# Value quads in the first layer, one-by-one takeover of accumulators, and eight adjoining runs of quads in the down projections

## The chip, the cores and the metric

The kernel runs on one core of one Trainium2 chip. The metric is the time on the device in microseconds: the median of three runs before the change is 2054.72 us (2054.33 to 2054.86).

TensorE (PE in the profile) multiplies; VectorE (DVE) and ScalarE (ACT) prepare what it reads and take over what it sums up in its eight PSUM banks; SyncE (SP) and GpSimd (POOL) issue most of the transfers.

## What is computed

Two transformer layers on 256 tokens of width 2048, in float32. The first layer has block-sparse attention, which for 256 tokens is plain causal attention in one block; the second has sliding-window attention with grouped keys and values. Both have a convolutional feed-forward network of inner width 5504.

```python
q, k, v = jnp.split(x @ w_qkv, 3, axis=-1)      # first layer, 2048 -> 3 x 2048
...
h = layer_norm(ALPHA * h + attn, ln_g[layer, 0], ln_b[layer, 0])
ffn = conv_ffn(h, ffn_w_up[layer], ffn_conv_w[layer], ffn_conv_b[layer], ffn_w_down[layer])
h = layer_norm(ALPHA * h + ffn, ln_g[layer, 1], ln_b[layer, 1])
...
return (jax.nn.gelu(g) * v) @ w_down            # 5504 -> 2048, at the end of conv_ffn
```

## The kernel before

**Products in three parts.** Every float32 operand is split into a high part that TensorE takes at its fast rate and a low remainder. A product of a 128-row block with a 512-column block is three matmuls (L530 to L532: high by high, high by low, low by high).

**The weight stream.** Weights come as *halves* of 128 x 1024 numbers (512 KB), all in one fixed sequence through all stages. SP loads a half into one of six `raw` buffers (L141). ACT copies its high part to `wh` (L160), DVE subtracts to get `wl` (L169), and when that is done the next load is issued. Four pairs `wh`, `wl` exist, so a half's split can begin when PE has finished the half four before it. Splits are called three halves ahead of their use.

**Stages.** For each layer: the attention's projections with the attention itself between them (value groups of 512 columns, and a unit for each head's query and key), the output projection, the up projection (86 units), the down projection. A stage with moving weights takes its output in two *chunk pairs* c = 0, 1 of 2 x 512 columns each (n = 0, 1 and n = 2, 3) and two token tiles t = 0, 1.

**Quads.** A *plain* half holds two weight blocks, each used for both token tiles: 4 block products, 12 matmuls. A *quad* treats 2 row blocks by 2 column blocks by 2 token tiles as a 2 x 2 product and needs 7 products instead of 8. A *run* is two quads in 7 halves of two products each (the list `SEVEN`); four of the seven hold weight blocks as they are, the halves that begin with T1 and T2 hold sums of weight blocks. `PLAINS` and `PLAINS_O` give the number of plain halves between the runs. A pair with quads uses all eight banks: four `acc` banks for (n, t) and four `at` banks for P1, P5, P6, P7, which `fold` adds up afterwards with DVE.

**Sums of weights** are made ahead by `presums`: two loads of 512 KB, four DVE steps (L436) and two stores to DRAM through POOL (L440) per quad, at given *slots*. **Sums of the source** are made on the spot by `sums`: `whole` (L588), `combine` (L599), `split` (L604, L605).

**What sets the order.** The engines run their own lists in the order in which the program writes them. The program counts slots: `step` closes one, `at(n, f)` puts `f` n slots later, and those actions are written at the next `take` of a half, right behind the splits called there. In the down projections a slot is one half.

**Ends of chunks and stages.** `evac` takes a finished bank into the residual `res` (L547, L549) and the last part of a (t, n) is followed by statistics (L553). Here it is called when both token tiles of an n are done. The last eight halves of a stage are the *window*: all eight for t = 0, then all eight for t = 1, so that the norm of t = 0 (`moments`, `norm`, L611 to L623) and its transposes (`turn`, L632, and `low`, L639) run beside the second pass. For this the window's splits are kept in spare places (`homes`, in `xT`, `st` and `up`), and in layer 0's down projection a table `reach` calls the splits further and further ahead, up to six halves of the next stage.

## Time and profile before

| | |
|---|---|
| median of three runs | 2054.72 us |
| the profiled execution | 2053.82 us |
| its span, first to last instruction | 2052.1 us |
| granted TensorE clock | 0.998 |
| `wl` splits on DVE (L169), one of 128 x 1024 | 1223 ns |
| `wh` splits on ACT (L160), one of 128 x 1024 | 1054 ns |
| quad steps ahead (L436), one of 224 | 685 ns |
| moved by DMA | 566.64 MB, mean 276 GB/s |

The profile is one execution, read by an engine's busy time, by the wait that ended an idle time, and by the granted clock. A matmul's row lasts about 390 ns, but matmuls overlap: the distance from one start to the next is the rate. Rows of the profile are named by line and operation, output and inputs; the line numbers are those of the kernel before.

### The profile page before, as it was taken

What the parts mean: (1) busy time and instruction counts of PE and PEld (TensorE: products, weight loads), DVE (VectorE), ACT (ScalarE), POOL (GpSimd) and SP (SyncE); (2) the same over time, 40 slices, a digit from 0 to 9 for tenths busy, and PEclk for the clock granted to TensorE, in tenths of its full rate; (3) what the DMA queues carried; (4) which work ended last, traced back from release to release, by engine and by line L of the source; (5) the groups of instructions that cost most, each with busy time, mean ns of one, the idle gap of its engine ahead of it and who ended that gap; (6) DMA issues with size and microseconds to landing.
All of it is one profiled execution on the core that took longest, in us unless ns stands there. A gap on an engine that the chain in (4) does not pass through costs nothing.

```text
span 2052.1 us, 29718 instructions
## 1 busy us (share of the span) xinstructions
PE 2036.1 (99%) x10908; PEld 1759.3 (86%) x10908; DVE 1675.9 (82%) x2399; ACT 1138.3 (55%) x1676; POOL 75.4 (4%) x138
## 2 busy tenths in 40 slices
PE   9999999999999999999999999999999999999997
PEld 7888888988888888888888888898888888888886
DVE  5676678888888888899896788978888888889887
ACT  5444456455555555566673556545555555556672
POOL 0100000000000000000000000000000000000000
PEclk9999999999999999999999999999999999999999
DMA  8888988468888888888994767838888888889893
GB/s 297 287 281 328 320 287 313 162 238 282 289 288 273 282 296 269 285 286 329 323 366 156 261 217 252 285 126 275 281 286 283 279 283 291 272 266 328 312 361 150
DMA packets 158722, 566.64 MB, mean 276 GB/s; under 512 B 19008, under 2 KB 21376, under 8 KB 157296
## 3 DMA queue, kind: packets, MB, share of 16 engines
q1 hardware_dynamic: 136064, 492.74, 70.7%
q0 software_dynamic: 20160, 69.64, 8.7%
q10 hardware_dynamic: 2352, 2.36, 0.3%
q8 instruction: 86, 1.41, 0.3%
q14 instruction: 60, 0.49, 0.1%
HBM read 503.78 MB, written 65.06 MB: 277 GB/s over the span
## 4 chain that ended last, share of the span: by engine, by line
PE 98%; DVE 1%; DMA 0%; ACT 0%; issue 0%; ACTq 0%; DVEq 0%
PE acc L322 39%; PE acc L324 20%; PE acc L530 7%; PE acc L531 7%; PE acc L532 7%; PE at L532 2%; PE at L531 2%; PE at L530 2%; PE acc L386 2%; PE acc L385 2%; PE acc L387 2%; PE acc L349 1%; PE acc L361 1%; PE at L722 1%; PE at L755 1%; PE at L748 1%
## 5 line engine op out<-in xcount | busy, mean ns | idle before, releaser
L169 DVE TENSOR_TENSOR wl<-raw,wh 128x1024 fp32r<-128x1024 f32 (+1 forms) x754 | 898.8, 1220 | 186.4 <-ACT wh L160 163.9
L160 ACT ACTIVATE wh<-raw 128x1024 fp32r<-128x1024 f32 (+1 forms) x754 | 770.4, 1052 | 207.9 <-PE acc L532 104.5
L322 PE MATMUL acc<-xT,wh 128*128 128x512 f32 x3456 | 832.8, 392 | 0.0
L322 PEld LDWEIGHTS acc<-xT,wh 128*128 128x128 f32 x3456 | 641.1, 188 | 128.6
L324 PEld LDWEIGHTS acc<-xT,wl 128*128 128x128 f32 x3456 | 444.2, 190 | 12.4
L324 PE MATMUL acc<-xT,wl 128*128 128x256 f32 x3456 | 452.5, 284 | 0.0
L909 ACT ACTIVATE h<-acc 128x256 f32<-128x256 f32 x172 | 66.4, 386 | 409.1 <-PE acc L324 203.1
L917 DVE SCALAR_TENSOR_TENSOR c<-h,cw,c 128x255 f32<-128x255 f32 x344 | 165.4, 481 | 9.1 <-ACT c L913 2.8
L436 DVE TENSOR_TENSOR gb<-gb 128x512 f32<-128x512 f32 x224 | 153.5, 685 | 5.9 <-DMA gb<-in_wsum_dram 5.9
L910 DVE TENSOR_TENSOR h<-acc,h 128x256 f32<-128x256 f32 x172 | 72.7, 423 | 64.2 <-ACT h L909 64.2
L440 POOL DMA_DIRECT2D ws<-gb x112 | 59.8, 534 | 1412.1 <-DVE gb L436 1360.3
L530 PE MATMUL acc<-wh,up 128*128 128x512 f32 x275 | 107.0, 389 | 0.0
L531 PE MATMUL acc<-wl,up 128*128 128x512 f32 x275 | 107.0, 389 | 0.0
L532 PE MATMUL acc<-wh,up 128*128 128x512 f32 x275 | 107.0, 389 | 0.0
L913 ACT ACTIVATE c<-h,cw 128x256 f32<-128x256 f32 x172 | 101.7, 591 | 0.0
L530 PE MATMUL acc<-wh,st 128*128 128x512 f32 x174 | 68.8, 395 | 0.0
L531 PE MATMUL acc<-wl,st 128*128 128x512 f32 x174 | 67.8, 390 | 0.0
L532 PE MATMUL acc<-wh,st 128*128 128x512 f32 x174 | 67.8, 390 | 0.0
L831 ACT ACTIVATE qT<-acc 128x256 f32<-128x256 f32 x32 | 12.3, 385 | 91.3 <-PE acc L324 65.9
L532 PEld LDWEIGHTS acc<-wh,up 128*128 128x128 f32 x275 | 51.6, 188 | 10.7
L530 PEld LDWEIGHTS acc<-wh,up 128*128 128x128 f32 x275 | 51.6, 188 | 10.7
L531 PEld LDWEIGHTS acc<-wl,up 128*128 128x128 f32 x275 | 51.6, 188 | 10.6
(193 smaller groups left out, 2152.5 us busy)
## 6 DMA issues: line engine op xcount, KB each, us to landing
raw<-in_wst_dram SPq DMA_DIRECT2D x694, 512.0 KB, 5.2
gb<-in_wsum_dram SPq DMA_DIRECT2D x112, 512.0 KB, 7.6
ws<-gb POOLq DMA_DIRECT2D x112, 512.0 KB, 6.2
raw<-ws SPq DMA_DIRECT2D x112, 512.0 KB, 5.6
bias<-band POOLq DMA_DIRECT2D x8, 512.0 KB, 7.2
band<-ud POOLq DMA_DIRECT2D x4, 512.0 KB, 12.7
band<-ud ACTq DMA_DIRECT2D x4, 512.0 KB
res<-in_x_dram SPq DMA_DIRECT2D x2, 1024.0 KB, 9.4
```

The costliest lines, as they stand in the source:

```text
L160: nc.scalar.activation(wh[:, c], raws[s][:, c], AF.Copy)
L169: nc.vector.tensor_tensor(out=wl[:, c], in0=raws[s][:, c], in1=wh[:, c].bitcast(F32), op=ALU.subtract)
L322: nc.tensor.matmul(acc, w, xT[:, k, :], start=(k == 0), stop=(k == ends[0]))
L324: nc.tensor.matmul(acc[:, 0:T], w, xT[:, k, 0:T], start=False, stop=(k == ends[1]))
L436: nc.vector.tensor_tensor(out=w[:, o:o + 512], in0=a, in1=b, op=op)
L530: nc.tensor.matmul(acc, sh, wh, start=first, stop=False)
L531: nc.tensor.matmul(acc, sh, wl, start=False, stop=False)
L532: nc.tensor.matmul(acc, sl, wh, start=False, stop=last)
L909: nc.scalar.activation(h, acc[:, T:2 * T], AF.Copy)
L910: nc.vector.tensor_tensor(out=h, in0=acc[:, 0:T], in1=h, op=ALU.add)
L913: nc.scalar.activation(c, h, AF.Identity, bias=w[:, 3:4], scale=w[:, 2:3])
L917: nc.vector.scalar_tensor_tensor(c[:, d:T], h[:, 0:T - d], w[:, 2 - d:3 - d], c[:, d:T], op0=ALU.mult, op1=ALU.add)
```

## The change

**Value quads.** In the first layer the third and fourth value groups are taken as one chunk pair by the new `v_pair`, with two runs of quads as in an output projection (8 plain halves and 14 of runs, 22 in place of 16). Its source sums go to rows of `st` that are still unused. Four more quads are summed ahead for it.

**Down projections.** In the second chunk pair there are eight runs instead of six, one behind the other, and then 11 plain halves (before: 42 halves of runs with 4 plain ones between, then 15 plain). The source sums of the two new runs are made within this chunk pair, at slots 9, 12, 14 and 15 and again 14 slots later, and are written over the blocks of runs 4 and 5, which therefore come first. Of the 11 plain halves eight are the window. Eight more quads are summed ahead; those of the down projections are now nearly all made during the up projections (26 and 27 of them, before 20 and 20), about every 6 slots instead of 8.

**Takeover.** `evac` is called for each (n, t) as it is done, and at slot distance 0, or 1 for t = 1 of odd n in the down projections (before: 1 and 2 for odd n). Since n = 2 now reaches into the window, `late` takes it over there.

The helpers of quads (`target`, `product`, `fold`, `sums`) move unchanged into a function `mixed` that both stages call; `sums` can be asked for `split` in two actions. The diff is cut to its core, without what only moved:

```diff
+MORE = 4
+RUNS = (range(6), (4, 5, 0, 1, 2, 3, 6, 7))
-PLAINS = ((5, 2, 2, 2, 2, 0, 6), (0, 1, 1, 1, 1, 0, 15))
+PLAINS = ((5, 2, 2, 2, 2, 0, 6), (0, 0, 0, 0, 0, 0, 0, 0, 11))
...
+PLAN_V = _mixed(1, PLAINS_O, _plain(range(KB - 2 * NQ_O), (2, 3)), KB // 2 - NQ_O)
-PLAN_DOWN = [h for c in range(2) for h in _mixed(c, PLAINS[c], _plain(range(2 * NQ, FT), (2 * c, 2 * c + 1)), 0)]
+PLAN_DOWN = [h for c in range(2) for h in _mixed(c, PLAINS[c], _plain(range(2 * (NQ + MORE * c), FT), (2 * c, 2 * c + 1)), 0, RUNS[c])]
...
-    QUADS[2 * _l + 1] = [(2 * _l + 1, c, p) for c in range(2) for p in range(NQ)]
+    QUADS[2 * _l + 1] = [(2 * _l + 1, c, p) for c in range(2) for p in range(NQ + MORE * c)]
+QUADS[4] = [(4, 1, KB // 2 - NQ_O + p) for p in range(NQ_O)]
-AHEAD_OF = {0: QUADS[0] + QUADS[1][:8], 1: QUADS[1][8:] + QUADS[2], 2: QUADS[3][:4], 3: QUADS[3][4:]}
+AHEAD_OF = {0: QUADS[4] + QUADS[0] + QUADS[1][:2], 1: QUADS[1][2:], 2: QUADS[2] + QUADS[3][:1], 3: QUADS[3][1:]}
...
-        presums(AHEAD_OF[2 * l], 3 if l else 22, 8 if l else 6)
+        if l == 0:
+            ahead = AHEAD_OF[0]
+            presums(ahead, [*range(16, 41, 6), *range(70, 95, 6)])
+        else:
+            presums(AHEAD_OF[2], range(3, 35, 7))
...
-            presums(AHEAD_OF[2 * l + 1], 4, 8)
+            ahead = AHEAD_OF[2 * l + 1]
+            presums(ahead, [156 * i // (len(ahead) - 1) for i in range(len(ahead))])
...
+        def place(i):
+            if 2 * i < NQ:
+                return xsum(i, ns)
+            flat = quad_blocks(RUNS[1][i - NQ // 2]).rearrange("p a b -> p (a b)")
+            return flat.rearrange("p (h q s c) -> p h q s c", h=2, q=2, s=4)
...
+            if ns == 3:
+                for i in range(MORE // 2):
+                    for j, f in zip((9, 12, 14, 15), sums(NQ // 2 + i, True)):
+                        at(whole + 14 * i + j, f)
...
         def late(t, i):
             last = i == WINDOW - 1
+            for n in range(NCH - 1):
+                if (n, t) not in evacuated and done((n, t)):
+                    evacuated.add((n, t))
+                    evac(n, t)
...
             for n in range(NCH):
-                if n not in evacuated and done((n, 0), (n, 1)):
-                    evacuated.add(n)
-                    for t in range(2):
-                        at((t + 1) * (n % 2), evac, n, t)
+                for t in range(2):
+                    if (n, t) not in evacuated and done((n, t)):
+                        evacuated.add((n, t))
+                        at(t * (n % 2) * (ns == 3), evac, n, t)
...
+        def v_pair():
+            src = lambda k: xT[:, k, :]
...
+            parted = mixed(src, PLAN_V, k0 // 2, lambda i: 4, lambda i: xT[:, k0 + 4 * i:k0 + 4 * i + 4, :], place, into)
+            mv = Moving(src, 0)
+            for i in range(len(PLAINS_O) - 1):
+                for j, f in enumerate(parted.sums(i)):
+                    at(sum(PLAINS_O[:i]) + 7 * i + j, f)
+            evacuated = set()
+            for half in PLAN_V:
+                blocks = [mv.block() for _ in range(2)]
+                for e, w in zip(half, blocks):
+                    for tgt in parted.target(e):
+                        parted.product(*tgt, *w)
+                step()
+                for n in (2, 3):
+                    for t in range(2):
+                        if (n, t) not in evacuated and parted.done((n, t)):
+                            evacuated.add((n, t))
+                            at(0, lambda n=n, t=t: into(t, n, parted.banks.pop((n, t))))
+            parted.fold(1)
+            run(before)
+            return vts
...
-                vt = v_group()
+                if g < 2:
+                    vt = v_group()
+                elif g == 2:
+                    vts = v_pair()
+                if g >= 2:
+                    vt = vts[g]
```

Three places of VectorE's list. The first is where layer 0's down projection passes from chunk pair 0 to 1: `res` from `acc` is the takeover of (1, 0) and (1, 1), `wl` from `raw` is the split of a half. Before the change VectorE's list reads:

```order
L547 TENSOR_TENSOR res_140<-res_140,at_8660 128x512
L169 TENSOR_TENSOR wl_9411<-raw_9303,wh_9410 128x1024
L169 TENSOR_TENSOR wl_9429<-raw_9315,wh_9428 128x1024
L169 TENSOR_TENSOR wl_9447<-raw_9328,wh_9446 128x1024
L169 TENSOR_TENSOR wl_9461<-raw_9348,wh_9460 128x1024
L547 TENSOR_TENSOR res_140<-res_140,acc_8687 128x512
L553 BN_STATS stats_8512<-res_140 128x6
L169 TENSOR_TENSOR wl_9477<-raw_9371,wh_9476 128x1024
L547 TENSOR_TENSOR res_140<-res_140,acc_9004 128x512
L553 BN_STATS stats_8512<-res_140 128x6
L169 TENSOR_TENSOR wl_9493<-raw_9392,wh_9492 128x1024
```

The changed kernel has at this place:

```order
L629 TENSOR_TENSOR res_152<-res_152,at_8758 128x512
L179 TENSOR_TENSOR wl_9509<-raw_9401,wh_9508 128x1024
L179 TENSOR_TENSOR wl_9527<-raw_9414,wh_9526 128x1024
L179 TENSOR_TENSOR wl_9545<-raw_9427,wh_9544 128x1024
L629 TENSOR_TENSOR res_152<-res_152,acc_8785 128x512
L635 BN_STATS stats_8610<-res_152 128x6
L179 TENSOR_TENSOR wl_9561<-raw_9446,wh_9560 128x1024
L629 TENSOR_TENSOR res_152<-res_152,acc_9102 128x512
L635 BN_STATS stats_8610<-res_152 128x6
L179 TENSOR_TENSOR wl_9577<-raw_9469,wh_9576 128x1024
L179 TENSOR_TENSOR wl_9591<-raw_9490,wh_9590 128x1024
```

Each takeover stands one split earlier. The second place is nine to fifteen halves on: the sum of source blocks for the first of the two new runs (L537 `whole`, L548 `combine`, L558 the low part), where before only splits stood. VectorE's list in the changed kernel:

```order
L179 TENSOR_TENSOR wl_9652<-raw_9580,wh_9651 128x1024
L179 TENSOR_TENSOR wl_9664<-raw_9594,wh_9663 128x1024
L537 TENSOR_TENSOR tmp_9669<-up_3141 128x1024
L179 TENSOR_TENSOR wl_9678<-raw_9607,wh_9677 128x1024
L179 TENSOR_TENSOR wl_9690<-raw_9619,wh_9689 128x1024
L179 TENSOR_TENSOR wl_9702<-raw_9631,wh_9701 128x1024
L548 TENSOR_TENSOR tmp_9669<-tmp_9669 128x2x128 x4
L179 TENSOR_TENSOR wl_9718<-raw_9643,wh_9717 128x1024
L179 TENSOR_TENSOR wl_9730<-raw_9655,wh_9729 128x1024
L179 TENSOR_TENSOR wl_9743<-raw_9667,wh_9742 128x1024
L558 TENSOR_TENSOR up_3141<-tmp_9669,up_3141 128x1024
L179 TENSOR_TENSOR wl_9756<-raw_9681,wh_9755 128x1024
```

Six operations of the new sum stand among the splits of the dense stretch; the same follows 14 splits later. The third place is the end of the first pass over the window in layer 0: the last operations of `fold` (L549, L547 with `at`), splits into `wl` and `up`, takeovers with statistics. Before the change VectorE has here:

```order
L547 TENSOR_TENSOR res_140<-res_140,acc_9456 128x512
L553 BN_STATS stats_8512<-res_140 128x6
L547 TENSOR_TENSOR res_140<-res_140,acc_9488 128x512
L553 BN_STATS stats_8512<-res_140 128x6
L169 TENSOR_TENSOR wl_10170<-raw_10106,wh_10169 128x1024
L169 TENSOR_TENSOR wl_10176<-raw_10110,wh_10175 128x1024
L169 TENSOR_TENSOR wl_10195<-raw_10114,wh_10194 128x1024
L169 TENSOR_TENSOR wl_10201<-raw_10130,wh_10200 128x1024
L169 TENSOR_TENSOR up_3091<-raw_10134,up_3091 128x1024
L169 TENSOR_TENSOR up_3091<-raw_10150,up_3091 128x1024
L547 TENSOR_TENSOR res_140<-res_140,acc_9498 128x512
L553 BN_STATS stats_8512<-res_140 128x6
```

In the changed kernel the same stretch, from the end of the fold on, reads:

```order
L631 SCALAR_TENSOR_TENSOR res_152<-res_152,tmp_10256 128x512 x2
L629 TENSOR_TENSOR res_152<-res_152,at_9568 128x512
L179 TENSOR_TENSOR wl_10328<-raw_10248,wh_10327 128x1024
L179 TENSOR_TENSOR wl_10334<-raw_10259,wh_10333 128x1024
L179 TENSOR_TENSOR up_3141<-raw_10263,up_3141 128x1024
L179 TENSOR_TENSOR up_3141<-raw_10283,up_3141 128x1024
L629 TENSOR_TENSOR res_152<-res_152,acc_9556 128x512
L635 BN_STATS stats_8610<-res_152 128x6
L629 TENSOR_TENSOR res_152<-res_152,acc_9596 128x512
L635 BN_STATS stats_8610<-res_152 128x6
L642 BN_AGGR ag_10399<-stats_8610 128x2
L696 RECIPROCAL rs_10403<-sd_10401 128x1
```

The fold, which before stood six splits ahead of the first row shown, now stands right before the splits of the next stage; the second takeover before the moments is now n = 3's, since that of n = 2, t = 1 has moved behind the norm.

More of the change, by code (lines that the diff above doesn't have):

```diff
@@ L2 @@
 from contextlib import ExitStack
+from types import SimpleNamespace
 import numpy as np
@@ L59, in _plain, with _mixed @@
     return [tuple(blocks[i:i + 2]) for i in range(0, len(blocks), 2)]
-def _mixed(c, groups, plain, p0):
+def _mixed(c, groups, plain, p0, runs=None):
     plan, at = [], 0
@@ L519, in project_out @@
-        for half in plan:
-            for e in half:
-                for key in keys(e):
-                    owed[key] = owed.get(key, 0) + 1
-        def product(key, sh, sl, wh, wl):
-            if key not in banks:
-                banks[key] = psum.tile([P, 512], F32, name="at" if key[0] in SUMS else "acc")
-                used[key] = 0
-            acc, first, last = banks[key], used[key] == 0, used[key] == owed[key] - 1
-            used[key] += 1
-            nc.tensor.matmul(acc, sh, wh, start=first, stop=False)
-            nc.tensor.matmul(acc, sh, wl, start=False, stop=False)
-            nc.tensor.matmul(acc, sl, wh, start=False, stop=last)
@@ L534, in done @@
-        def done(*keys):
-            return all(used.get(key) == owed[key] for key in keys)
         def zs(t, n):
             return res[:, t, n * 512:(n + 1) * 512]
+        def place(i):
[3 more added lines that the diff above has]
+            return flat.rearrange("p (h q s c) -> p h q s c", h=2, q=2, s=4)
+        parted = mixed(src, plan, p0, lambda i: ns + (2 * i >= NQ), quad_blocks, place, lambda t, n, a: into(t, n, a))
@@ L540, in project_out @@
+        banks, target, product, done, fold, sums = (parted.banks, parted.target, parted.product, parted.done, parted.fold,
+                                                    parted.sums)
         paired = {e[2] for half in plan for e in half if e[0] == "B11"}
```

184 lines of the change are left out of this document (115 added, 69 removed).

## The prediction

> **What bounds the kernel now.** I read the page first: its busy times, then the chain of work that ended last.
>
> ```profile
> span 2052.1 us, 29718 instructions
> PE 2036.1 (99%) x10908; PEld 1759.3 (86%) x10908; DVE 1675.9 (82%) x2399; ACT 1138.3 (55%) x1676; POOL 75.4 (4%) x138
> PE 98%; DVE 1%; DMA 0%; ACT 0%; issue 0%; ACTq 0%; DVEq 0%
> ```
>
> TensorE is nearly the whole chain, so fewer matmuls shorten the kernel wherever the others can still feed it. VectorE's 82% is a mean over stages; the stages decide, so I asked for 50 us windows (columns: PE, weight load, DVE, ACT, POOL busy with counts, granted clock, DMA share, GB/s).
>
> ```profile
> 300.00:350.00 50.00, 49.50 (x223) 40.69 (x221) 44.37 (x55) 33.17 (x39) 1.60 (x3) 1.00 0.91 328
> 450.00:500.00 50.00, 50.00 (x281) 43.82 (x280) 41.60 (x66) 27.68 (x45) 2.13 (x4) 1.00 0.85 294
> 950.00:1000.00 50.00, 49.62 (x219) 40.79 (x218) 45.03 (x46) 31.68 (x31) 0.00 (x0) 1.00 0.90 327
> 1250.00:1300.00 50.00, 49.51 (x225) 40.77 (x224) 44.57 (x60) 33.42 (x43) 0.00 (x0) 1.00 0.77 262
> 1850.00:1900.00 50.00, 50.00 (x221) 41.17 (x220) 46.70 (x47) 35.61 (x35) 0.00 (x0) 1.00 0.93 321
> 1900.00:1950.00 50.00, 49.62 (x220) 40.72 (x218) 43.47 (x45) 30.27 (x30) 0.00 (x0) 1.00 0.87 312
> 1000.00:1050.00 50.00, 50.00 (x223) 41.39 (x222) 41.81 (x35) 36.11 (x34) 0.00 (x0) 1.00 0.97 356
> ```
>
> Three things are to be seen. In a down projection (1850 to 1900) PE does 221 matmuls of 128x512 in 50 us: 0.226 us each, so a run's half (6 of them) lasts 1.36 us and a plain half (12) 2.72. PE's only idle time in mid-kernel is 0.5, 0.38, 0.49 and 0.38 us in four windows. And DVE there is busy 93% (46.70 of 50), so it has little left to give.
>
> **What is removed.** The plans give the count. A run of quads needs 14 block products in 7 halves where 4 plain halves need 16. The value pair goes from 64 products to 60, each down projection from 160 to 156. That is 12 products of 3 matmuls, 36 x 0.226 = **8.1 us** less PE work. The halves go from 808 to 826, so ACT, DVE and the DMA queue each get 18 more to prepare.
>
> **Hidden work.** Twelve more quads are summed ahead, four DVE steps each.
>
> ```profile
> L436 DVE TENSOR_TENSOR gb<-gb 128x512 f32<-128x512 f32 x224 | 153.5, 685 | 5.9 <-DMA gb<-in_wsum_dram 5.9
> L588 DVE TENSOR_TENSOR tmp<-up 128x1024 f32<-128x1024 f32 x4 | 4.9, 1218 | 0.0
> L599 DVE TENSOR_TENSOR tmp<-tmp 128x256 f32<-128x256 f32 x52 | 20.6, 421 | 0.7
> L605 DVE TENSOR_TENSOR xT<-tmp,xT 128x1024 fp32r<-128x1024 f32 x4 | 4.9, 1223 | 0.0
> ```
>
> The up projection of layer 0 lies between these two rows of the chain in order of time:
>
> ```profile
> 405.18 7.68 PE acc L361 x64
> 861.14 7.09 PE acc L322 x31
> ```
>
> There 6 or 7 more quads mean at most 7 x 4 x 0.685 = 19 us of DVE over some 460 us, 2 us on the 41.60 in the 450 to 500 window. PE stays the bound there: cost 0. If that cover went, it would be at most those 19 us per layer, but it would need DVE to lack 8 us in 50, which that row contradicts. The SP loads of a quad queue ahead of later weights, and its steps wait for them; before, such waits are 5.9 us in the whole trace and none reaches PE. The value pair has the same 22 halves, in the same order, as the first chunk pair of an output projection, where PE loses 0.5 us in all (window 300 to 350), and behind it come matmul units with DVE to spare. I bound its stall by 0 and 1 us and take 0.
>
> **Taking over accumulators one by one.** The output projections' idle 0.5 us is bank (0,0) waiting to be read. It is now read two halves earlier, but (0,1) still ends with the last product, 3 matmuls before its bank is wanted, so I count half: 0.5 us for both layers. Bounds: 0 and 1.0. The down projections' 0.38 us each go too, **0.8**, but their cause moves, as the next rows show.
>
> **The feed of a run without plain halves.** Four buffers hold split weights; ACT starts on one when PE has freed it.
>
> ```profile
> 1034.29 1.06 ACT L160 ACTIVATE wh<-raw 128x1024 fp32r<-128x1024 f32 x1 [0.30 <-PE acc L532]
> 1040.83 2.59 DVE L169 TENSOR_TENSOR wl<-raw,wh 128x1024 fp32r<-128x1024 f32 x2
> 1044.97 0.39 PE L530 MATMUL at<-wh,xs 128*128 128x512 f32 x1
> ```
>
> The second split of the DVE row ends at 1043.42, and PE begins on that half at 1044.97: a lead of **1.55 us**. It is the same for every half of a dense stretch, because the next split must wait for PE (0.30 + 1.06 + 1.22 after a buffer is freed). So a dense stretch can take 1.55 us of other DVE work, plus 0.23 since only PE's second matmul reads `wl`. The chunk change shows what happens beyond that (layer 1, DVE and PE rows):
>
> ```profile
> 1931.54 2.59 DVE L169 TENSOR_TENSOR wl<-raw,wh 128x1024 fp32r<-128x1024 f32 x2 [1.35 <-ACT wh L160]
> 1934.04 0.68 DVE L547 TENSOR_TENSOR res<-res,acc 128x512 f32<-128x512 f32 x1
> ...
> 1934.10 0.39 PE L532 MATMUL acc<-wh,st 128*128 128x512 f32 x1
> 1934.87 0.47 PE L530 MATMUL acc<-wh,xT 128*128 128x512 f32 x1 [0.38 <-DVE res L547]
> 1936.49 0.68 DVE L547 TENSOR_TENSOR res<-res,acc 128x512 f32<-128x512 f32 x1
> 1937.21 0.69 DVE L553 BATCH_NORM_STATS2 stats<-res 128x6 f32<-128x512 f32 x1
> 1937.82 5.75 DVE L169 TENSOR_TENSOR wl<-raw,wh 128x1024 fp32r<-128x1024 f32 x5
> ```
>
> Two evacuations with statistics cost DVE 1.33 us each (1936.49 to 1937.82). Back to back, splits come every 1.13 us ((5.75 - 1.22) / 4), so a late DVE regains 1.36 - 1.13 = 0.23 us per half, as long as the raw weights are there.
>
> Now the evacuations stand a split earlier. The bank is free by 1933.4 and PE, due 0.23 after its start at 1934.10, need not wait for it. But the splits go on from 1931.54 + 1.14 = 1932.68: evacuation, split, evacuation, split end at 1932.68 + 1.33 + 1.14 + 1.33 + 1.22 = 1937.70, where PE wants that half at 1934.33 + 2 x 1.36 = 1937.05: 0.65 less the 0.23 is a new stall of 0.4. Then there is no plain half for some 50 more, and two new sums (for quads 6 and 7) fall into them: 1.14 + 4 x 0.38 + 1.14 = 3.8 us of DVE each. Before the first the lead has grown back to about 1.4 us; with 6 halves among its pieces (1.4) and the 0.23, it is 0.8 short. The second finds 1.5 and is 0.7 short. That makes 0.4 + 0.8 + 0.7 = 1.9 us per layer. If raw weights come only every 1.25 us (below), recovery is 0.11, the shortfalls are 2.3 and 2.2, and it is 4.9. The rows right after a delay run at 1.13, so I take **2.2**, near that end; for two layers 4.4 (bounds 3.8 and 9.8).
>
> **The turnover of layer 0.** From a point some 6 halves ahead of the last plain halves, splits go into spare homes and DVE runs freely, through 16 splits, the fold of the pair, 6 splits of the next stage and the evacuations, to the moments of token tile 0.
>
> ```profile
> 1043.56 1.23 DVE L169 TENSOR_TENSOR xT<-raw,xT 128x1024 fp32r<-128x1024 f32 x1
> 1047.69 0.39 PE L530 MATMUL acc<-st,up 128*128 128x512 f32 x1
> 1048.62 3.73 DVE L169 TENSOR_TENSOR wl<-raw,wh 128x1024 fp32r<-128x1024 f32 x3
> 1052.27 0.69 DVE L549 SCALAR_TENSOR_TENSOR res<-res,tmp 128x512 f32<-128x512 f32 x1
> 1068.54 0.68 DVE L547 TENSOR_TENSOR res<-res,acc 128x512 f32<-128x512 f32 x1
> 1069.86 0.67 DVE L547 TENSOR_TENSOR res<-res,acc 128x512 f32<-128x512 f32 x1
> 1075.71 2.36 DVE L169 TENSOR_TENSOR up<-raw,up 128x1024 fp32r<-128x1024 f32 x2
> 1077.98 0.68 DVE L547 TENSOR_TENSOR res<-res,acc 128x512 f32<-128x512 f32 x1
> 1080.90 0.75 DVE L623 SCALAR_TENSOR_TENSOR res<-res,rs,gb 128x512 f32<-128x512 f32 x1
> 1083.06 0.60 PE L632 MATMUL at<-ident,res 128*128 128x128 f32 x4
> ```
>
> Before, this DVE chain takes from 1043.5 to 1077.98 = 34.5 us with hardly a gap, and PE's first pass over the window (7 plain halves from 1047.69, then 8 of 1.36) ends at 1047.69 + 19.04 + 10.88 = 1077.6: the two meet to 0.4 us. The normalized first columns are ready at 1081.65 and PE transposes them at 1083.06, so 1.4 us is the slack. Now PE has 3 plain halves where it had 7: 10.9 us less. The dense halves ahead absorb 4 splits and start the free stretch at the same lead, 6 halves ahead of the first plain one (9.7 us against 4.2 before). So PE's pass ends 9.7 + 8.16 + 10.88 = 28.7 us after DVE's start. The chain has the same 22 splits and fold; one evacuation (1.32) moves behind the norm: 34.5 - 1.3 = 33.2. DVE is 33.2 - 28.7 - 0.4 = 4.1 us late. Less 1.4 of slack, PE stalls 2.7 at the transpose, and about 0.6 more at the next stage's first low halves, which stand behind the moved evacuation: **3.3**. Queued behind are eight norms and the four transposes, which keep PE's own pace once shifted. Bounds: 1.5 (if the splits ahead start sooner) and 5 (if the 1 MB load of the bias row, now in the dense part, holds raw weights back). Layer 1 has no next stage and pays nothing here.
>
> **The sum**, against the profiled execution (2053.82 us, span 2052.1): 2053.8 - 8.1 - 0.5 - 0.8 + 4.4 + 3.3 = 2052.1. The median of the three runs shown, 2054.72, is 0.9 above that execution, so I predict **2053.0**. A measurement tells about 0.2% from no change, so "same" is 2050.6 to 2058.8.
>
> **Rivals.** (1) *PE stays the bound.* If the turnover's chain is shorter than I count and dense stretches stall by their lower bound only, the time is 2054.7 - 9.4 + 3.8 = 2049.1; with no stall at all 2045.3. For it: PE ran through DVE at 93% without a gap. Against: the 0.4 us at which chain and pass meet at 1077.98, and a lead of 1.55 us against pieces of 3.8.
>
> (2) *The weight stream becomes the bound*, and the change is slower. A half is 524,288 bytes; at 1.36 us that is 385 GB/s. It decides from there: the 356 GB/s of the window 1000 to 1050 would give 1.47 us, 0.11 more for each of 56 + 8 halves, 7 us less 1.5 of lead, 5.5 per layer. DVE's shortfalls would hide in that, the turnover not: 2054.7 - 9.4 + 11 + 3.3 = 2059.6. For it: the DMA share 0.97 in that window. Against:
>
> ```profile
> 1044.00:1056.00 12.00, 12.00 (x54) 9.93 (x54) 11.65 (x12) 10.62 (x11) 0.00 (x0) 1.00 1.02 418
> ```
>
> where splits run free the stream gives 418 GB/s, 1.25 us a half (the 3.73 us of three splits at 1048.62 agree). The 356 also held plain halves, which need less.
>
> The Trainium skill, "DMA: Bandwidth & Descriptors", section "Where 436 GB/s comes from", says that for transfers between HBM and SBUF the HBM side, about 358 GB/s per core, binds. By that rule this rival would be the outcome, near 2059. The trace disagrees with it: 418 GB/s was sustained for 12 us with one core running, so I give the rule little weight.
>
> (3) *DVE regains only 0.11 per half*: 4.9 instead of 2.2 per layer, 2058.4.
>
> **How the numbers follow.** Forecast (2050.6 to 2057) 0.52, of which 0.06 falls below 2050.6; rival 1 0.30 (0.27 faster); rival 2 0.10 (0.06 slower); rival 3 0.08 (0.03 slower). Faster 0.33, same 0.58, slower 0.09. The range 2047.5 to 2058.5 leaves out a gain with hardly a stall (about 0.09) and the upper half of rivals 2 and 3 (about 0.09). The forecast's own range stands beside it because a third of the chance is on the faster side.
>
> **What would show it.** In the profile after: 0.226 us a matmul still, and 36 fewer; no idle time at the value pair; PE idle of about 2 us spread over three or four places in each second chunk pair, ended by DVE's splits; a gap of about 3 us ended by DVE's norm just before the transposes behind layer 0's down projection. If PE's gaps there end on ACT waiting for raw weights, rival 2 is right. If the second gap is absent, the chain of 34.5 us was not as rigid as its rows look. The prediction fails as a whole if the stalls in up projections, which I cost at nothing, appear.

## The result, and the profile after

| | before | after |
|---|---|---|
| median | 2054.72 us (2053.83 to 2055.28, 5 runs) | 2072.37 us (2070.88 to 2072.74, 5 runs) |
| ratio, with its 95% interval | | 1.0084 (1.0073 to 1.0094) |
| profiled execution, and its span | 2053.82, 2052.1 | 2072.23, 2070.4 |

The change makes the kernel slower by 17.7 us, outside the predicted range. Two of all the executions in this document, one of f1 below and one of the kernel before that was timed beside it, ran at a granted clock of 0.65, took 2884 and 2895 us and are left out. The page of the changed kernel (busy times, then the shares of the chain):

```profile
span 2070.4 us, 30029 instructions
PE 2038.4 (98%) x10872; PEld 1755.8 (85%) x10872; DVE 1746.6 (84%) x2509; ACT 1163.1 (56%) x1701; POOL 88.2 (4%) x162
PE 86%; DMA 7%; DVE 4%; issue 1%; ACT 1%; POOL 0%; SPq 0%; ACTq 0%; DVEq 0%
```

The 36 matmuls are gone (10872), yet PE holds 86% of the chain where it held 98; transfers and VectorE have the rest. The 50 us windows, in the columns of the prediction, say where:

```profile
300.00:350.00 50.00, 50.00 (x229) 41.42 (x228) 43.97 (x54) 32.60 (x39) 2.13 (x4) 1.00 0.86 305
450.00:500.00 50.00, 50.00 (x292) 44.26 (x292) 43.45 (x69) 27.67 (x45) 3.20 (x6) 1.00 0.89 313
1000.00:1050.00 50.00, 46.74 (x197) 36.05 (x196) 46.58 (x46) 36.47 (x36) 0.00 (x0) 1.00 0.94 343
1050.00:1100.00 50.00, 43.90 (x190) 35.98 (x189) 45.25 (x49) 30.73 (x32) 0.00 (x0) 0.96 0.90 348
1250.00:1300.00 50.00, 50.00 (x254) 42.46 (x254) 43.65 (x77) 31.34 (x55) 2.66 (x5) 1.00 0.78 275
1950.00:2000.00 50.00, 46.80 (x198) 36.22 (x197) 46.66 (x47) 35.29 (x34) 0.00 (x0) 1.00 0.91 317
```

The output projections (300, 1250) have lost their 0.5 us of idle time and the up projection (450) has no stall. The second chunk pairs (1000, 1950) hold 197 and 198 matmuls where the window from 1000 held 223. PE's waits, with total, times and the longest, name three places:

```profile
PE at L501 <- DVE wl L179: 7.0, 16, 1.1
PE at L663 <- DVE res L654: 6.1, 1, 6.1
PE at L787 <- DVE L L782: 5.3, 1, 5.3
```

The first two are the dense chunk pairs and the turnover. The third lies in layer 0's attention, which the prediction never looked at. The chain in order of time shows how it comes about:

```profile
71.20 14.59 DMA band<-ud
85.79 0.30 issue
86.09 0.46 POOL bias L311
86.55 0.32 issue
86.86 8.45 DMA ws<-gb
95.31 0.02 issue
95.33 0.69 DVE gb L446
96.03 0.09 DVE rsm L780
96.11 0.03 issue
96.14 0.30 DVE L L782
96.43 0.04 issue
96.48 0.95 PE at L787 x3
```

POOL issues in order. Its `bias` load waits for a transfer until 85.79; the two stores of the first quad's sums stand behind it and go out at 86.86. VectorE's next quad step (L446) overwrites what they read, so it waits until they land, and behind it stand the softmax and PE's transposes. Before, the presums began six slots later; the timeline of POOL has there:

```profile
82.73 0.78 POOL L301 DMA_DIRECT2D bias<-band  x1 [13.14 <-DMA band<-ud]
91.68 0.55 POOL L440 DMA_DIRECT2D ws<-gb  x1 [8.16 <-DVE gb L436]
```

The store came 9 us after the `bias` load and waited for VectorE alone. And a wait leaves something behind. Windows of the changed kernel around this place, then around the turnover:

```profile
91.20:96.40 5.20, 0.00 (x0) 0.00 (x0) 1.03 (x4) 1.06 (x1) 0.00 (x0) 0.92 0.67 268
95.60:102.40 6.80, 5.92 (x16) 4.68 (x17) 4.52 (x8) 0.49 (x1) 0.54 (x1) 0.50 0.54 157
102.50:110.00 7.50, 7.50 (x36) 6.25 (x35) 3.58 (x5) 3.45 (x4) 0.53 (x1) 1.00 0.86 284
1095.70:1102.50 6.80, 5.59 (x17) 4.64 (x18) 6.62 (x11) 1.19 (x2) 0.00 (x0) 0.50 0.06 22
```

After both idle times the granted clock is 0.50 for some 6.8 us: 16 and 17 matmuls where 7.50 us at full clock hold 36.

### The profile page after: what moved, and what is told of

It reads as the page before. It is cut to its first block, busy times and chain, and to the rows that moved or that the text cites. A ratio compares the mean times of both kernels' runs of the same rounds, so it can differ in the third digit from the quotient of the medians.

```text
span 2070.4 us, 30029 instructions
## 1 busy us (share of the span) xinstructions
PE 2038.4 (98%) x10872; PEld 1755.8 (85%) x10872; DVE 1746.6 (84%) x2509; ACT 1163.1 (56%) x1701; POOL 88.2 (4%) x162
## 4 chain that ended last, share of the span: by engine, by line
PE 86%; DMA 7%; DVE 4%; issue 1%; ACT 1%; POOL 0%; SPq 0%; ACTq 0%; DVEq 0%
PE acc L332 37%; PE acc L334 19%; PE acc L500 6%; PE acc L501 6%; PE acc L502 6%; DMA band<-ud 3%; DVE wl L179 2%; DMA raw<-in_wst_dram 2%; DMA raw<-ws 2%; PE at L501 2%; PE at L502 2%; PE at L500 2%; PE acc L359 1%; PE acc L371 1%; ACT wh L170 1%
## 5 line engine op out<-in xcount | busy, mean ns | idle before, releaser
L179 DVE TENSOR_TENSOR wl<-raw,wh 128x1024 fp32r<-128x1024 f32 (+1 forms) x772 | 918.0, 1219 | 159.8 <-ACT wh L170 142.6
L170 ACT ACTIVATE wh<-raw 128x1024 fp32r<-128x1024 f32 (+1 forms) x772 | 788.8, 1053 | 193.5 <-PE acc L502 85.7
L446 DVE TENSOR_TENSOR gb<-gb 128x512 f32<-128x512 f32 x272 | 186.2, 685 | 7.2 <-DMA ws<-gb 7.2
L450 POOL DMA_DIRECT2D ws<-gb x136 | 72.6, 534 | 1398.4 <-DVE gb L446 1287.0
L501 PE MATMUL acc<-wl,up 128*128 128x512 f32 x244 | 95.1, 390 | 0.0
L500 PE MATMUL acc<-wh,up 128*128 128x512 f32 x244 | 95.0, 389 | 0.0
L502 PE MATMUL acc<-wh,up 128*128 128x512 f32 x244 | 94.9, 389 | 0.0
L501 PEld LDWEIGHTS acc<-wl,up 128*128 128x128 f32 x244 | 45.8, 188 | 9.8 <-DVE wl L179 0.3
L500 PEld LDWEIGHTS acc<-wh,up 128*128 128x128 f32 x244 | 45.8, 188 | 9.5
L502 PEld LDWEIGHTS acc<-wh,up 128*128 128x128 f32 x244 | 45.8, 188 | 9.4
```

The costliest lines, as they stand in the source:

```text
L170: nc.scalar.activation(wh[:, c], raws[s][:, c], AF.Copy)
L179: nc.vector.tensor_tensor(out=wl[:, c], in0=raws[s][:, c], in1=wh[:, c].bitcast(F32), op=ALU.subtract)
L446: nc.vector.tensor_tensor(out=w[:, o:o + 512], in0=a, in1=b, op=op)
L450: nc.gpsimd.dma_start(wsums[q][:, js], w[:, js])
L500: nc.tensor.matmul(acc, sh, wh, start=first, stop=False)
L501: nc.tensor.matmul(acc, sh, wl, start=False, stop=False)
```

## The experiments

Each run was compared with the kernel before on its own chip, whose median lay between 2054.12 and 2054.97. As a measure of the dense part I use the matmuls in the 60 us window 985 to 1045: 267 before, 238 after; each one fewer is 0.226 us lost there.

### The queue on POOL, and the clock

**a1_slot22**: presums later, one quad fewer ahead of the output projection.

```diff
-AHEAD_OF = {0: QUADS[4] + QUADS[0] + QUADS[1][:2], 1: QUADS[1][2:], ...
+AHEAD_OF = {0: QUADS[4] + QUADS[0] + QUADS[1][:1], 1: QUADS[1][1:], ...
-            presums(ahead, [*range(16, 41, 6), *range(70, 95, 6)])
+            presums(ahead, [*range(22, 41, 6), *range(70, 95, 6)])
```

> The first layer's weight sums start at slot 22 as before the change, with one quad fewer ahead of the output projection (it moves to the up projection). Theory (the value quads' stores queue on POOL behind the bias rows, VectorE waits 7.2 us for one, PE 5.3, and the clock halves behind that idle time): the wait of VectorE and the idle time at 91 to 96 us go, and with them the halved clock that follows it; 5.3 + about 3 less, near 2064. Rival (the value pair and its four quads cost their VectorE and DMA work wherever they stand): the time stays within 2 us of 2072.

Measured: 2063.35 us (2063.09 to 2063.78), 9.0 less; the wait at L787 is gone.

**a2_store_sp**: slots as in the change, but the first quad's stores on another queue.

```diff
-            nc.gpsimd.dma_start(wsums[q][:, js], w[:, js])
+            (nc.sync if q == ORDER[0] else nc.gpsimd).dma_start(wsums[q][:, js], w[:, js])
```

> Only the two stores of the first quad go through SP's queue in place of POOL's; slots stay at 16. Theory (POOL's order of issue is the cause, not the slot): VectorE no longer waits 7.2 us for a store, PE's 5.3 us and the halved clock behind them go, near 2064 as with slot 22. Rival (the earlier slot costs VectorE or the DMA queues something of itself): PE still idles 3 us or more between 85 and 100 us. If the stores hold back weights on SP's queue, PE idles elsewhere by 1 to 3 us.

Measured: 2064.63 us, 7.7 less. Same slot, same work, no wait at L787: it was the place in POOL's queue. One wait of 0.3 us appears at 187 us instead.

**c3_fill_att**: the changed kernel, with TensorE kept busy while it waits.

```diff
             S["pt"] = pt = at_tile()
+            if l == 0 and h == 3:
+                for _ in range(34):
+                    nc.tensor.transpose(pt[:, 0:P], ident, ident)
```

> The changed kernel itself (2072.37 us) with 34 dummy transposes of the identity on TensorE ahead of the transposes at 91 to 96 us in layer 0's attention, where it idles 5.3 us. VectorE and the store it waits for are untouched. Theory (idle time halves the granted clock for 6.83 us and that costs about 3 us on top of the wait): the wait stays, the matmuls behind it run at 0.23 us again, 2069 to 2070. Rival (the halved clock has another cause, or costs nothing in the end): 2071.5 or more.

Measured: 2068.91 us (2067.53 to 2070.56), 3.5 less. Nothing that TensorE waits for came sooner; the window behind the wait now reads:

```profile
96.00:103.00 7.00, 6.11 (x29) 5.06 (x30) 6.01 (x10) 1.82 (x3) 0.54 (x1) 1.00 0.49 160
```

Not all of the 3.5 us belongs to this place, since later stages differ from execution to execution. The rows tell what does. From the first transposes behind the wait to the products at L794 the changed kernel goes from 96.48 (in the chain above) to

```profile
102.34 0.64 PE L794 MATMUL at<-PT,vt 128*128 128x256 f32 x2
```

and c3, where the same products stand at L797:

```profile
96.89 0.70 PE L790 MATMUL at<-ident,L 128*128 128x128 f32 x3 [1.99 <-DVE L L782]
100.18 0.59 PE L797 MATMUL at<-PT,vt 128*128 128x256 f32 x2
```

That is 5.86 us against 3.29: the halved clock costs 2.6 us here, on top of a wait of 5.3.

### The dense second chunk pairs

**a3_no_sums**: the changed kernel without the sums of the two new runs.

```diff
             if ns == 3:
                 for i in range(MORE // 2):
-                    for j, f in zip((9, 12, 14, 15), sums(NQ // 2 + i, True)):
-                        at(whole + 14 * i + j, f)
+                    pass
```

> Leaves out the source sums of the two new runs in both layers (their sum blocks hold other numbers); matmuls, splits and loads are as in the change. Theory (VectorE's 3.8 us of sums among dense splits make the stalls): PE's idle time in the dense second chunk pairs falls from about 6 to about 1 us per layer, time near 2062. Rival (raw weights come too slowly for 56 dense halves, whoever works on VectorE): at least 4 us of stalls per layer stay and the time is above 2068.

Measured: 2064.11 us (2059.16 to 2067.98, a wide spread), 8.3 less; 257 matmuls in the window, and PE's wait for `wl` falls from 7.0 to 1.4 us. In both layers' windows (985 and 1945) it has 33 matmuls more than the changed kernel, 7.5 us. It fits the theory, but so would anything that makes a small delay grow.

**c2_spread**: on a1, the same sums, farther apart.

```diff
-                    for j, f in zip((9, 12, 14, 15), sums(NQ // 2 + i, True)):
-                        at(whole + 14 * i + j, f)
+                    for j, f in zip(((8, 16, 24, 25), (32, 40, 46, 47))[i], sums(NQ // 2 + i, True)):
+                        at(whole + j, f)
```

> On top of the kernel with slot 22 (2063.35 us): the same sums of the two new runs, in pieces about eight halves apart (slots 8, 16, 24, 25 and 32, 40, 46, 47 in place of 9, 12, 14, 15 and 23, 26, 28, 29). VectorE does the same work in these 56 halves. Theory (stalls come because the pieces stand closer than the lead grows back, 0.11 to 0.2 us per half): the dense stalls, 3.4 to 5.5 us per layer, fall to 1 to 2; time 2057 to 2060. Rival (the amount of work decides, wherever it stands in the dense part): stalls as before, 2062 or more.

Measured: 2063.25 us (a1 has 2063.35). My theory failed: eight halves between the pieces gain nothing.

**c1_seven_runs**: on a1, seven runs, one sum in distant pieces, 15 plain halves behind.

```diff
-MORE = 4
-RUNS = (range(6), (4, 5, 0, 1, 2, 3, 6, 7))
-PLAINS = ((5, 2, 2, 2, 2, 0, 6), (0, 0, 0, 0, 0, 0, 0, 0, 11))
+MORE = 2
+RUNS = (range(6), (4, 5, 0, 1, 2, 3, 6))
+PLAINS = ((5, 2, 2, 2, 2, 0, 6), (0, 0, 0, 0, 0, 0, 0, 15))
...
-                    for j, f in zip((9, 12, 14, 15), sums(NQ // 2 + i, True)):
+                    for j, f in zip((9, 21, 32, 33), sums(NQ // 2 + i, True)):
```

> On top of the kernel with slot 22: seven adjoining runs in the second chunk pairs and 15 plain halves behind them (in place of eight and 11); the sum of the one new run is made in pieces 11 to 12 halves apart (slots 9, 21, 32, 33 in place of 9, 12, 14, 15). Theory (adjoining runs keep a lead of 1.56 us when nothing else stands on VectorE, a piece of 1.1 to 1.5 us fits into it, and it grows back by some 0.11 per half; with 15 plain halves the turnover keeps its lead): no stall in the dense part beyond 0.5 us, no turnover gap, 12 matmuls fewer than with six runs: 2049.1 - 2.7 = 2046.4 (2045.8 to 2047.5). Rival (49 halves of 1.36 us without a plain one outrun the weight stream by themselves): 2049 or more.

Measured: 2055.51 us (2052.77 to 2058.82), 9 above the theory. ScalarE's timeline shows what it waits for:

```profile
1000.76 1.06 ACT L170 ACTIVATE wh<-raw 128x1024 fp32r<-128x1024 f32 x1 [1.53 <-DMA raw<-ws]
1002.28 1.06 ACT L170 ACTIVATE wh<-raw 128x1024 fp32r<-128x1024 f32 x1 [0.46 <-PE acc L502]
1003.53 1.06 ACT L170 ACTIVATE wh<-raw 128x1024 fp32r<-128x1024 f32 x1 [0.19 <-DMA raw<-in_wst_dram]
1005.54 1.06 ACT L170 ACTIVATE wh<-raw 128x1024 fp32r<-128x1024 f32 x1 [0.95 <-DMA raw<-ws]
```

Raw weights are late. From 965 to 1050 ScalarE waits 7.2 us in all for halves from `ws`, the store of summed halves, and 6.5 us for plain ones, which come through the same queue. (Of the seven halves of a run the four that begin with T1 and T2 are read from this store and three are weight blocks as they are; the description of quads ahead of the prediction says four for the latter.)

**d1_seven_pool**, **d3_eight_pool**: the sums on GpSimd (d1 on c1, d3 on c2).

```diff
+            eng = nc.gpsimd if apart else nc.vector
...
-                    nc.vector.tensor_tensor(out=o, in0=a, in1=b, op=op)
+                    eng.tensor_tensor(out=o, in0=a, in1=b, op=op)
```

The other two operations of `sums` change in the same way.

> The kernel with seven adjoining runs (2055.51 us), with the source sum of the new run made by GpSimd in place of VectorE, at the same slots; ACT's part stays. Theory (VectorE's 3.8 us delay its splits, each load waits for a split, and the stream that runs at 1.25 us of 1.36 cannot win the time back): the dense stalls, 4.4 and 2.8 us, fall to the 0.45 us of the chunk change and at most 0.5 more, the lead into the turnover is whole again and the gap of 2 us there goes: 2046.5 to 2050. Rival (49 halves of 1.36 us outrun the weight stream whatever VectorE does, or GpSimd's operations slow VectorE's by as much): 2053 or more.

> The kernel with eight adjoining runs and spread sums (2063.25 us), with both sums on GpSimd. Theory (as for seven runs): dense stalls of 4.3 to 5 us per layer fall to about 1; the turnover gap of 5 us or more stays, since its plain halves are 11; 2055 to 2058. Rival (the stream): 2061 or more.

Measured: 2056.50 us (2055.51 with VectorE) and 2072.22 us (2063.25). No relief, but also no clean test. The timelines of VectorE and GpSimd in d1 lie side by side:

```profile
973.06 6.37 DVE L179 TENSOR_TENSOR wl<-raw,wh 128x1024 fp32r<-128x1024 f32 x3
...
972.57 2.41 POOL L538 TENSOR_TENSOR tmp<-up 128x1024 f32<-128x1024 f32 x1 [106.37 <-DVE res L632]
975.06 5.66 POOL L549 TENSOR_TENSOR tmp<-tmp 128x256 f32<-128x256 f32 x4
```

Three splits that take 3.73 us in a row elsewhere take 6.37 beside GpSimd's operations. The Trainium skill, "SBUF — State Buffer", section "SBUF: two separate sides", says that VectorE and GpSimd share a port pair which one holds for a whole instruction while the other is blocked; for a VectorE operation with two inputs in SBUF, as a split is, it says so only beside a GpSimd operation that reads SBUF. The trace agrees, with 2.6 us more for three splits.

**e1_two_tiles**: on c1, each stored half as a tensor of its own.

```diff
-    wsums = {q: dram.tile([P, 2 * HW], F32, name="ws" + "_".join(map(str, q))) for q in ORDER}
+    wsums = {q: [dram.tile([P, HW], F32, name="ws" + "_".join(map(str, (*q, j)))) for j in range(2)] for q in ORDER}
...
-        return wst[f] if isinstance(f, int) else f[0][:, f[1] * HW:(f[1] + 1) * HW]
+        return wst[f] if isinstance(f, int) else f[0][f[1]]
...
-            nc.gpsimd.dma_start(wsums[q][:, js], w[:, js])
+            nc.gpsimd.dma_start(wsums[q][j], w[:, js])
```

> The kernel with seven adjoining runs (2055.51 us, sums on VectorE), with the stored sums of weights of a quad in two DRAM tensors of 128 x 1024 in place of one of 128 x 2048, so that each half is one piece of 512 KB as the plain weights are. Background: in the runs the halves from this store land 1.6 us after the half before them on average, others 1.25 to 1.4, and the DMA engines are 0.96 busy at 354 GB/s, where plain halves move at 418. Theory (rows of 4 KB at a pitch of 8 KB are slower to read): they land every 1.25 us, dense stalls 4.4 and 2.8 us fall to 1, time 2047 to 2050. Rival (it is the place or the time of issue, not the layout): 2054 to 2057 as before.

**e2_other_source**: on c1, the same bytes from the plain weights.

```diff
-                source.append((wsums[li, half[0][2], half[0][1]], j))
+                if li % 2 and half[0][2]:
+                    source.append(taken - 60 - j)
+                else:
+                    source.append((wsums[li, half[0][2], half[0][1]], j))
```

> The same kernel with seven runs, but in the second chunk pairs of the down projections the 28 halves of stored sums are loaded from earlier halves of the plain weights instead (other numbers, same bytes; the sums are still made and stored). Theory (reading the store is what slows the stream, by layout or by place): dense stalls fall to about 1 us per layer and the turnover gap of 2 us goes, 2047 to 2050. Rival (the stream falls behind because loads are issued late, whatever they read): 2054 or more.

Measured: 2049.75 us (2048.89 to 2051.69) and 2050.77 us (2049.33 to 2053.80). The window 985 to 1045, first with the store's old layout (c1):

```profile
985.00:1045.00 60.00, 57.03 (x245) 45.22 (x244) 51.40 (x48) 42.99 (x42) 0.00 (x0) 1.00 0.96 354
```

then with the store in two tensors (e1):

```profile
985.00:1045.00 60.00, 59.60 (x263) 48.87 (x262) 55.63 (x51) 46.17 (x45) 0.00 (x0) 1.00 0.99 377
```

The DMA engines were busy in both (0.96 and 0.99), but move 354 and 377 GB/s. In c1 rows of 4 KB are read at a pitch of 8 KB; in e1 a half is one piece. e1 still reads the store and gains 5.8 us, e2 reads other memory and gains 4.7: what was slow was the store in its old form, not a store as such, nor the time of issue. With VectorE's sums in both, 5.8 us of 2055.5 came from how the store is laid out. In e1 the pitch, the addresses and the number of tensors change together; that it is the pitch is the likeliest reading, not shown by itself.

**f1_eight_two_tiles**: the same three lines on a1, with eight runs.

> The kernel with slot 22 and eight adjoining runs (2063.35 us, sums at 9, 12, 14, 15 and 14 later, bias row as in the change), with the stored sums in two DRAM tensors per quad. Theory (the store's layout made the dense part outrun the stream; VectorE's sums and the 11 plain halves at the turnover cost on top of it): dense stalls of 5.5 and 3.4 us fall to 1 to 2.5 each, the turnover gap shrinks by the lead that is kept (about 1 us) but stays above 3, 2054 to 2058. Rival (with eight runs VectorE's sums alone make the stalls): less than 2 us better, 2061.5 or more. Second rival (the layout was all of it): 2050 or less.

Measured: 2058.87 us (2057.80 to 2060.76), 4.5 less; 250 matmuls in the window (a1 243, the changed kernel 238), and the wait at the turnover is still 5.4 us. With eight runs the layout is part of it: sums and turnover remain.

### The turnover of layer 0

Its end in the changed kernel, on ScalarE, VectorE and PE:

```profile
1079.70 1.06 ACT L170 ACTIVATE st<-raw 128x1024 fp32r<-128x1024 f32 x1 [3.29 <-DMA raw<-in_wst_dram]
1080.79 1.23 DVE L179 TENSOR_TENSOR st<-raw,st 128x1024 fp32r<-128x1024 f32 x1 [1.48 <-ACT st L170]
...
1089.60 2.35 DVE L179 TENSOR_TENSOR up<-raw,up 128x1024 fp32r<-128x1024 f32 x2
1091.87 0.68 DVE L629 TENSOR_TENSOR res<-res,acc 128x512 f32<-128x512 f32 x1
1092.59 0.69 DVE L635 BATCH_NORM_STATS2 stats<-res 128x6 f32<-128x512 f32 x1
1093.19 0.67 DVE L629 TENSOR_TENSOR res<-res,acc 128x512 f32<-128x512 f32 x1
...
1096.91 1.12 PE L663 MATMUL at<-ident,res 128*128 128x128 f32 x4 [6.10 <-DVE res L654]
```

**a4_no_fold** (on the change), **b1_gb_early** and **b2_gb_early_no_fold** (on a1; b2 takes both edits):

```diff
-                    fold(c)
+                    if li == 1 and c == 1:
+                        for b in SUMS:
+                            banks.pop((b, c))
+                        for tn in ((0, 2), (0, 3), (1, 2), (1, 3)):
+                            parts[tn] = 1
+                    else:
+                        fold(c)
...
-                at((whole - 4, len(plan) - WINDOW - 5)[i], load_gb, i)
+                at((whole - 4, whole - 2)[i], load_gb, i)
```

> Leaves out the fold of the second chunk pair in layer 0's down projection (about 5 us of VectorE), nothing else. Theory (the chain on VectorE from the free stretch to the moments is too long for PE's shortened pass): the idle time of 6.1 us at 1091 falls to 1 us or less and the halved clock at 1096 is gone, time near 2063 to 2064. Rival (late raw weights or the bias row's load set that gap): the gap shrinks by less than 2 us and the time stays above 2069.

> On top of the kernel with slot 22 (2063.35 us): the 1 MB load of the second bias row is issued two slots ahead of the chunk change, among plain halves, in place of five slots ahead of the window, in both down projections. Theory (the turnover gap of 5.8 us has two feeders, VectorE's chain with the fold and the stream of raw weights with the bias row in it; either alone holds most of it): the gap shrinks by 1 to 2.5 us, time 2061 to 2062.5. Rival (the row alone sets the gap): the gap falls below 2 us and the halved clock behind it goes, near 2056. Second rival (VectorE alone): no change.

> As the run with the early bias row, and the fold of layer 0's second chunk pair is left out. Theory (two feeders): with both taken away the gap falls to 1.5 us or less, the halved clock goes, time near 2056. Rival (the splits start the stretch behind PE because of the dense halves, and that alone is enough for a gap): a gap of 3 us or more stays, time above 2059.

Measured: PE's wait there is 4.7 us without the fold (2070.45 us), 5.9 with the early row (2061.82 us; a1 has 5.9 in two waits, the longer 5.6, and 2063.35 us), 2.3 with both (2058.19 us). Taking away 5 us of VectorE's chain shortened the wait by 1.4, because VectorE then waits for ScalarE, and that for a raw half that lands late behind the bias row. VectorE's timeline without the fold:

```profile
1077.94 1.23 DVE L179 TENSOR_TENSOR st<-raw,st 128x1024 fp32r<-128x1024 f32 x1 [3.06 <-ACT st L170]
```

Each of the two hides the other. That the raw half stands behind the bias row is read from the order of issue (the row at 1067.48, the late half behind it). What stays in b2 is not a lost start, as its rows show: from VectorE's first split into a spare place (1048.06) to the second takeover ahead of the moments (1080.10) it works 27.8 of 32.0 us, and its longest waits are 1.32 us for a late half from the store and 1.24 us behind ScalarE's table load (1071.75 to 1073.04). With the seven runs of e1 and 15 plain halves, which also give PE's pass its 10.9 us back, PE's wait is 0.4.

**b3_fill**: on a1, dummy transposes in this wait, as in c3.

> On top of the kernel with slot 22 (2063.35 us): 34 dummy transposes of the identity, some 5 us of TensorE, stand ahead of the first transposes behind layer 0's down projection, where PE idles 5.8 us for VectorE. Nothing comes sooner to VectorE. Theory (the granted clock halves for 6.83 us because TensorE idled, and costs about 2.5 us on top of the wait): the 0.5 clock behind the gap goes, 2060.5 to 2061.3. Rival (the halved clock comes from something else at this place, or its slow matmuls are hidden by the following waits): 2063 or more.

Measured: 2062.70 us (2058.96 to 2064.31) against 2063.35: by the times inconclusive, since runs with dense stalls scatter by more than the effect sought. The profiled execution, the lowest, kept the clock at 1.00, and its rows tell more. The first and the third group of transposes in a1:

```profile
1089.92 1.12 PE L663 MATMUL at<-ident,res 128*128 128x128 f32 x4 [5.63 <-DVE res L654]
1096.42 0.60 PE L663 MATMUL at<-ident,res 128*128 128x128 f32 x4
```

and in b3, behind the dummy transposes:

```profile
1086.73 0.66 PE L666 MATMUL at<-ident,res 128*128 128x128 f32 x4 [1.41 <-DVE res L654]
1090.44 0.60 PE L666 MATMUL at<-ident,res 128*128 128x128 f32 x4
```

The same work takes 6.50 us in a1, 6.31 in the changed kernel (1096.91 to 1103.22) and 3.71 in b3: here too the halved clock costs 2.6 to 2.8 us.

### The parts alone, and what can be kept

**b4_six_runs**: on a1, the second chunk pairs as before the change.

```diff
+MORE = 0
+RUNS = (range(6), range(6))
+PLAINS = ((5, 2, 2, 2, 2, 0, 6), (0, 1, 1, 1, 1, 0, 15))
```

> On top of the kernel with slot 22: the second chunk pair of the down projections has six runs with one plain half between and 15 behind, as before the change; the value quads and the one-by-one takeover stay. Theory (value pair and takeover cost nothing, all of the loss is in the adjoining runs and the turnover they shorten): 12 matmuls fewer are 2.7 us, takeover 0.5 to 1.3, so 2054.7 - 3.6 = 2051 (2050.5 to 2052). Rival (value quads are not free): 2053 or more.

Measured: 2049.14 us (2048.69 to 2049.80), ratio 0.9974 (0.9964 to 0.9984). Value quads and takeover are worth 5.6 us together. So 17.7 splits up: -5.6 for these, +9.0 for POOL's queue, +14.2 for the eight adjoining runs although they save 24 matmuls (5.4 us).

**d2_seven_pool_gb**: d1 with the early bias row.

> The same with the load of the second bias row two slots ahead of the chunk change, among plain halves. Theory (with VectorE's chain in step again the row is hidden by 15 plain halves, or holds the window back a little): 0 to 1 us below the run without it. Rival (the load delays the splits at the chunk change, where two takeovers already cost 0.45): 0.5 to 1.5 us above it.

Measured: 2056.03 us against 2056.50, within the scatter of both.

**f2_seven_one_plain**: e1 with the early bias row, one plain half after the third run, and the sum's low part later.

```diff
-PLAINS = ((5, 2, 2, 2, 2, 0, 6), (0, 0, 0, 0, 0, 0, 0, 15))
+PLAINS = ((5, 2, 2, 2, 2, 0, 6), (0, 0, 0, 1, 0, 0, 0, 14))
...
-                at((whole - 4, len(plan) - WINDOW - 5)[i], load_gb, i)
+                at((whole - 4, whole - 2)[i], load_gb, i)
...
-                    for j, f in zip((9, 21, 32, 33), sums(NQ // 2 + i, True)):
+                    for j, f in zip((9, 21, 32, 36), sums(NQ // 2 + i, True)):
```

> Seven runs, stored sums in two tensors (2049.75 us), and in addition one of the 15 plain halves stands after the third run, the sum's low part comes four halves after its high part, and the second bias row is loaded ahead of the chunk change. Theory (a plain half gives 1.36 us of lead where the sum's second piece stands; the bias row's share of the stream makes up for the plain half that the turnover loses): the stalls of 0.6 to 0.7 us at the pieces go, no turnover gap above 0.5 us, 2047.5 to 2049. Rival (the turnover needs all 15 halves): a gap of 1 us or more there, 2050 or more.

Measured: 2046.66 us (2046.15 to 2046.82), ratio 0.9958 (0.9945 to 0.9971), the fastest of all. Its dense window:

```profile
985.00:1045.00 60.00, 60.00 (x266) 49.72 (x265) 56.20 (x51) 46.71 (x45) 0.00 (x0) 1.00 0.98 375
```

PE has no gap with VectorE busy 56.20 of 60 us. Which of the three edits brought the 3.1 us over e1 was not tried.

## Why the prediction was wrong

**Less PE work, 8.1 us**: right. 36 matmuls fewer, at the same pitch.

**The takeover, 0.5 + 0.8 us**: right in kind. The idle times in the output projections are gone. Together with the value pair's 2.7 us it was to give 4.0; b4 measured 5.6. The output projections' two idle times were 1.0 us in all, and in b4 both are gone, where half was counted; the other 1.1 us were not traced.

**Hidden work, "cost 0"**: this step failed, by 9.0 us. It asked whether VectorE, PE and SP's queue had room, and for these it was right. It did not ask what the moved presums issue on POOL. The stores came to stand behind a `bias` load that was not yet released, so they landed late, and VectorE's next step may not overwrite their source before. The row that shows it, the `bias` load at 82.73 in the timeline of before, was there to be read. Of the 9.0 the wait itself is 5.3, and the rows of c3 put 2.6 on the granted clock, which the prediction left out entirely.

**The dense stretch, 2.2 us per layer**: the mechanism named (VectorE's sums use up the lead) has a large part: a3, without the sums, wins back 7.5 us. What failed is the step "a late DVE regains 0.23 us per half, as long as the raw weights are there", with the choice of its size, and with it the dismissal of rival 2. I took 418 GB/s from 12 us in which only plain halves were split, and let it stand for runs, where four of seven halves come from the store. There the raw weights are late, and the mean is 323 and 324 GB/s in the changed kernel, 354 in c1. In place of 4.4 us the changed kernel loses 11.8 (238 and 242 matmuls where b4 has 266, in the windows 985 to 1045 and 1945 to 2005, so 28 + 24 of 0.226), and a1 9.5 (243 and 247). Rival 3 (9.8, VectorE regains less because the weights come slower) and rival 2 (11, the stream is the bound) are both nearer in size; for eight runs the experiments do not decide between them. The layout alone is 2.5 us of it (f1 has 250 and 251). With a layout that lets the stream run at 371 to 377, seven runs are nearly free of stalls. Nor is there a fixed limit near the 356 GB/s that rival 2 worked with: e1 held 377 over 60 us.

**The turnover, 3.3 us**: right in place and chain (a gap before the transposes, ended by VectorE's norm), and right in VectorE's work: 32.7 us from its first split into a spare place (1057.68) to the second takeover ahead of the moments (1093.19), where the chain was put at 33.2. Wrong in size: 6.1 us, and a halved clock behind it that costs 2.6. The step that failed is that this chain would run with hardly a gap, as before. It takes 35.5 us, since VectorE waits in it, 1.48 us for the raw half behind the bias row and 0.65 for a half from the store. The step "start the free stretch at the same lead" nearly held: VectorE starts an estimated 9.2 us ahead of the first plain half (the last product of a run into `at` is at 1065.26; before the change that was at 1046.11 and the first plain half at 1047.69, 1.58 us on), where 9.7 was counted. The bound of 5 us for the bias row treated it as an alternative to the fold; b1 and b2 show that both chains run close together.

**The sum** was 2052.1 for a profiled execution of 2072.23. The 20 us between are 7.9 (the wait in the attention and its clock, 5.3 + 2.6), 7.4 (dense part, 11.8 against 4.4), 2.8 (turnover, 6.1 against 3.3) and 2.6 (the second halved clock). These make 20.7; the 1.6 that value pair and takeover gave beyond the forecast bring it to 19.1, and 1.0 stays open.

## What to carry to other kernels

When a step is moved, follow each transfer that it issues on its own queue, to what stands ahead of it there and to the step that must wait until it lands. Take a stream's rate from a stretch that reads the same things in the same layout; a busy share of 0.96 at 354 GB/s did not mean that no more could come: with another layout the engines moved 377. Where two chains end at one place within a few microseconds, an experiment that takes away one measures only their distance.

## What the hardware showed that was not expected

- Idle time on TensorE can cost twice. After 5.3 us the granted clock was 0.50 for some 6.8 us, which cost 2.6 us by the rows of c3. A wait of 2.3 us (1081.61 to 1083.90) sufficed too; the windows of b2 with it and behind it:

```profile
1081.38:1084.79 3.41, 1.12 (x8) 0.88 (x7) 2.94 (x7) 0.46 (x2) 0.00 (x0) 1.00 0.53 213
1084.79:1088.20 3.41, 3.41 (x11) 2.75 (x10) 3.34 (x6) 0.91 (x2) 0.00 (x0) 0.50 0.00 0
```

The Trainium skill, "TensorE: Matmul & The Clock Gate", section "What's actually happening", lets the clock fall after an idle window of about 3.4 us and rise after a busy one. The trace agrees with the two levels; the fall after 2.3 us is sooner than that, and the 6.8 us are twice the window.

The traces show a beat. In every run every stretch at one clock, from one change to the next, is a whole multiple of 3.413 us (in the changed kernel 88.75 us are 26 of them and 6.83 two, in b2 3.41 is one), and in b2 the 3.41 us just before the fall still hold 1.12 us of PE work. Pauses of 1.8 and 2.0 us (c1, c3) left the clock at 1.00, pauses of 2.3, 4.0 and 4.7 us (b2, a4) gave one halved stretch of 3.41 us, pauses of 5.2 us and more (c3 at the turnover, the changed kernel, a1) two. That a pause's place in the beat decides with its length fits this, but was not tried.

- Storing the sums as rows of 4 KB at a pitch of 8 KB, and not in pieces of 512 KB, cost 5.8 us in a kernel of 2055 us, though only 28 halves of 512 KB in each dense part are read from there (128 in the whole kernel). Where plain halves stood between the runs, the old layout cost nothing that shows (b4 has 266 matmuls in its window).
- An operation of GpSimd on 128 x 1024 numbers took 2.4 to 2.5 us, and three splits of VectorE beside two such stretches took 1.7 times theirs (6.37 against 3.73 us).
